# Hybrid decoder layer on one core: squares of x on two engines, S5 kernel blocks read inside the first rotation, S5 outputs copied by VectorE beside the o projection, one factor sum for two expert pairs

## The chip, the core and the metric

The kernel runs on one core of a Trainium2 chip. A core has a matrix engine (PE in the profile, with its weight loads as PEld), VectorE (DVE), ScalarE (ACT), GpSimd (POOL) and SyncE (SP, which here only starts transfers and waits). They share an on-chip memory; matrix results go to PSUM, eight banks of 128 partitions by 512 floats; DMA engines bring the weights from HBM. Each engine runs its own instructions in the order in which they were written and waits on semaphores for the others. The metric is the device time of the whole program in microseconds, lower is better.

## The reference, cut to what matters

One layer of a hybrid decoder, batch 1, 256 tokens, width 1024, all in float32.

```python
h    = rmsnorm(x, norm_mix_g)                       # (256, 1024)
p    = h @ w_in                                     # columns q | k | v | o (512 each) | i, f (4 each) | u (512)
A    = sigmoid(o) * headnorm(mlstm(silu(conv(q)), silu(conv(k)), v, i, f))      # 4 heads of 128
s_t  = abar * s_{t-1} + bbar @ u_t                  # S5: 32 groups of 16 channels, 64 complex states each
y    = gelu(Re(C s) + D u);  z = y @ glu_w + glu_b
B    = z[:16] * sigmoid(z[16:])                     # per group
x    = x + concat([A, B]) @ w_out
t    = rmsnorm(x, norm_ffn_g)
# top 1 of 4 groups, then top 2 of the 8 experts in it: weights combine[t, e]
x    = x + sum_e combine[:, e] * ((silu(t @ w_gate[e]) * (t @ w_up[e])) @ w_down[e])   # 32 experts, 1024 x 512
out  = rmsnorm(x, norm_final_g)
```

The 32 experts' weights are 201 MB of float32, and every one of them is read.

## The kernel before, in words

Nothing schedules the work: what is written first is issued first on each engine, and Python generators (`run` empties one, `next` takes one step) weave pieces of different parts into one order. `half(i)` is one of a set of 8 KB-per-partition slots of on-chip memory, `cst`, `mw` and `xs` are smaller areas, and `PS[:, bk, :]` is PSUM bank bk.

1. **Start.** x comes in two blocks of 128 tokens, `xs[:, 0]` and `xs[:, 1]`. Its squares are summed (L253 on VectorE for block 0; L262 and L263, one half each on VectorE and ScalarE, for block 1). GpSimd adds eps and takes the power -1/2 (L238 and L239 of `rpow`, then L265 and L266). PE transposes x meanwhile (L258), spreads the two factors over the columns (L275, L276), and VectorE writes the normalised, transposed h (L283). Projections that have h^T as the moving operand are `proj32T` (L433), with h as the stationary one `proj32N` (L441); u is the first of them.
2. **S5.** `transposeB(0)` and `(1)` (L494) transpose the input matrices four blocks at a time into a bank that VectorE, and for the fourth batch ScalarE, copies out (L497). `inputs_to_states` (L522, L524) and `kernelK` (L505) follow; the latter makes the blocks of the S5 kernel inside a chunk in bank 1. `rotate(0)` and `rotate(1)` (L577 to L597) turn the states of one half of the groups each, run the scans (L588) and turn them back (L589 to L597). Between them L600 to L603 read the kernel's blocks (`K4`, bank 1) into `KX`. `proj32N("v", (0, 1))` writes banks 0 and 1.
3. **mLSTM.** q, k, v and o are projected; `conv` does the short convolution (L531 on ScalarE, L535 on VectorE, SiLU L538). `prep` splits weights into a rounded high part (ScalarE, L422) and the rest (GpSimd or VectorE, L423), and `projN` makes a projection with three matmuls of the parts (L452, L454, L456) a quarter at a time, o into banks 5 and 7.
4. **S5 outputs.** `states_to_outputs` (L650) leaves the outputs transposed in banks 0 and 1; they are copied into `YT` (L703, one bank by ScalarE, the other by VectorE); `outputs_back` transposes them (L657) and ScalarE takes the GELU (L660). `glu(t)` is the per-group gate (L714 to L721). The scores (L666), `w_out` (L800), the residual, the second norm and the router follow.
5. **Experts.** They are done in 16 pairs. For each pair, one-hot matrices of the chosen tokens gather the inputs (L984), `wide` multiplies by gate, up and the last by down (L1011), `weigh` (L1017, L1018) scales and splits the result, and `scatter` (L1026) adds it into four banks. `factors` (L956 to L963) makes the gathered tokens' norm factors for the next pairs: two tiny matmuls and a sum over three columns per pair. It is called once for one pair and seven times for two.
6. **Weights.** `fetch(upto)` (L128 to L151) issues the expert weights on SyncE's queue (L150), 1 MB each for most, in the order of their use and into the slots that the steps before have freed; SyncE waits at each for the slot and for an older transfer.

Of the kernel before, what the change touches and what calls it, by code (L numbers as in the profile page):

```python
# [20 lines left out]
D = 1024  # L21
# [51 lines left out]
def tile_hymba(ctx, tc, x, norm_mix_g, w_in, conv_w, conv_b, i_bias, f_bias, mlstm_norm_g,  # L73
# [178 lines left out]
    flat = lambda t, c: t[:, c].rearrange("p b t -> p (b t)")  # L252
    STT(scr[:, 0, :], xs[:, 0, :], 1.0 / D, xs[:, 0, :], OP.mult, OP.mult, accum_out=ssq[:, 0:1])  # L253
    V.tensor_copy(ldt0[0:16], rowsA[0:16, 0:2])
# [5 lines left out]
    for _ in range(2):  # L260
        MM(PS[:, 0, 0:128], ident, ident, start=True, stop=True)
    STT(scr[:, 0, 0:512], xs[:, 1, 0:512], 1.0 / D, xs[:, 1, 0:512], OP.mult, OP.mult, accum_out=sh[:, 1, 0:1])  # L262
    ACT(scr[:, 1, 0:512], xs[:, 1, 512:], AF.Square, scale=1.0 / 32, accum_out=sh[:, 1, 1:2])  # L263
    rpow(ssq[:, 0:1], ssq[:, 0:1], 1.0, 1)
    G.tensor_scalar(ssq[:, 1:2], sh[:, 1, 0:1], sh[:, 1, 1:2], EPS, OP.add, OP.add)  # L265
    G.tensor_tensor(ssq[:, 1:2], ssq[:, 1:2], neg_half[:, 0:1], OP.pow)  # L266

    p = dict(zip(["dt", "lr", "lrdt", "mag", "th", "n", "r", "ab", "sin", "cos", "f", "hi", "lo", "den", "am1",
# [280 lines left out]
    load_w("o", (19, 21))  # L549
    for i in range(2):  # L550
        run(transposeB(i))
    run(inputs_to_states())
# [24 lines left out]
    def rotate(n):  # L577
        rs = slice(8 * n, 8 * n + 8)
        cT, sT, z, w = [t[:, rs] for t in (cosT, sinT, zr, zi)]
        a, b, c = [tt[:, i] for i in range(3)]  # L580
        TT(a, Vr[:, rs], cT, OP.mult)
        TT(b, Vi[:, rs], sT, OP.mult)
        TT(c, Vi[:, rs], cT, OP.mult)
        TT(w, Vr[:, rs], sT, OP.mult)
        TT(z, a, b, OP.add)
        TT(w, c, w, OP.subtract)
        for t in (z, w):
            V.tensor_tensor_scan(fl(t), fl(rho[:, rs]), fl(t), 0.0, OP.mult, OP.add)  # L588
        TT(a, z, cT, OP.mult)  # L589
        TT(b, w, sT, OP.mult)  # L590
        TT(c, z, sT, OP.mult)

        TT(z[:, :, 1:64], a[:, :, 0:63], b[:, :, 0:63], OP.subtract)
        TT(a, w, cT, OP.mult)
        TT(w[:, :, 1:64], a[:, :, 0:63], c[:, :, 0:63], OP.add)
        for t in (z, w):
            V.memset(t[:, :, 0:1], 0.0)  # L597

    rotate(0)
    TT(dd[0:32], fr(dsk[0:32], (1, 16), (0, 16)), fr(dl16[0:32], (0, 16), (1, 16)), OP.mult)  # L600
    TT(KX, fr(K4, (32, 16), (0, 2), (1, 16)), fr(mask2, (0, 16), (1, 2), (0, 16)), OP.mult)  # L601
    TT(dd2[0:32], fr(dd[0:32], (16, 16), (0, 2), (1, 16)), fr(mask2[0:32], (0, 16), (1, 2), (0, 16)), OP.mult)
    TT(KX[0:32], KX[0:32], dd2[0:32], OP.add)  # L603
    cv = conv(0, 2)
    qk = cuts(half(7), (8, 256))[0]
# [5 lines left out]
    prep(2)  # L611
    rotate(1)
    next(cv)
# [88 lines left out]
    for h in range(2):  # L702
        (V.tensor_copy if h else A.copy)(YT[:, h], PS[:, h, :].rearrange("p (q f) -> p q f", q=4))  # L703
    outputs_back()
# [24 lines left out]
    next(cv)  # L729
    for i in range(4):  # L730
        run(projN("o", (5, 7), i))
        if i == 0:
            for g in gated((0, 1)):
                run(g)
            for m in range(4):
                next(cv)
        if i == 1:
            next(cv)
        if i == 2:
            gl = gated((2, 3))  # L740
# [215 lines left out]
    def factors(js, bk):  # L956

        for j in js:
            at = PS[:, bk, 4 * j:4 * j + 3]
            for b in range(2):  # L960
                MM(at, oh[:, b, 2 * j:2 * j + 2].rearrange("p e s -> p (e s)"), rpt[:, b], start=b == 0, stop=b == 1,
                   skip_group_check=True)
            V.tensor_reduce(rp[:, j:j + 1], at, AX.X, OP.add)  # L963

# [376 lines left out]
```

## Time and profile before

| | |
|---|---|
| median of 3 runs | 615.29 us (614.74 to 617.84) |
| the profiled execution | 615.09 us |
| its span in the profile | 613.4 us, about 1.7 us lie around it |
| mean granted clock of PE | 0.992 |
| busy: PE, PEld, DVE, ACT, POOL | 582.2, 311.8, 226.4, 127.0, 58.1 us |
| chain that ended last | PE 90%, DVE 4%, ACT 2%, issue 1%, DMA 1%, POOL 1% |
| weights and rest read from HBM | 218.17 MB, 357 GB/s over the span |

The span runs from the first to the last instruction of the profiled execution, and all starts below are counted from it. The chain goes back from the last instruction, at each step to whatever released it. A timeline row gives start, duration and engine of one instruction, or of several of the same kind with their count, and in brackets how long the engine sat idle before it and what ended that. PE's records come in two per matmul of this precision, so an instruction of the program can be two records. Granted clock 1.00 is 2.4 GHz and 0.5 is 1.2 GHz.

### The profile page before, as it was taken

Reading aid. Unit: us, or ns where it says so; the run is one execution under the profiler, and the core shown is the slowest. Engines: PE = TensorE matmul, PEld = TensorE weight load, DVE = VectorE, ACT = ScalarE, POOL = GpSimd, SP = SyncE. Lnnn points to the kernel's source line nnn. Section 1 sums busy time; section 2 is a strip of 40 time slices with the busy share of each in tenths; the row PEclk is TensorE's granted clock in tenths of the full one; section 3 lists DMA queues with packets and bytes.
Section 4 is the critical chain, followed back from the end, with each engine's and each line's share of the span. In section 5 each row is a group of like instructions: output and inputs, shape, how many; then the busy total and the mean of one; then the engine's idle time right before and its main releaser. Section 6 shows DMA issues by size and latency. Waiting matters only on the chain.

```text
span 613.4 us, 8110 instructions
## 1 busy us (share of the span) xinstructions
PE 582.2 (95%) x3228; PEld 311.8 (51%) x3228; DVE 226.4 (37%) x589; ACT 127.0 (21%) x236; POOL 58.1 (9%) x74
## 2 busy tenths in 40 slices
PE   7999997999999999999999999999999999999993
PEld 6788486877743633363363335335433533444342
DVE  5969961685832311231322123132212313221133
ACT  3481647432411010000100010110001010101023
POOL 7040319050000000000000000000000000000003
PEclk9999998999999999999999999999999999999997
DMA  8791049299999999999999999999999999999992
GB/s 226 242 301 59 3 185 418 70 389 409 379 384 420 418 419 420 419 420 419 419 419 418 422 419 420 420 419 419 420 418 420 418 419 420 419 420 420 416 292 74
DMA packets 51337, 219.79 MB, mean 358 GB/s; under 512 B 15236, under 2 KB 20448, under 8 KB 27232
## 3 DMA queue, kind: packets, MB, share of 16 engines
q1 hardware_dynamic: 50800, 218.17, 88.7%
q10 hardware_dynamic: 496, 1.06, 0.5%
q8 instruction: 27, 0.44, 0.3%
q14 instruction: 14, 0.11, 0.0%
HBM read 218.17 MB, written 1.05 MB: 357 GB/s over the span
## 4 chain that ended last, share of the span: by engine, by line
PE 90%; DVE 4%; ACT 2%; issue 1%; DMA 1%; POOL 1%; POOLq 0%; DVEq 0%; ACTq 0%
PE psum L1011 55%; PE psum L984 6%; PE psum L433 6%; PE psum L1026 5%; PE psum L800 4%; PE psum L441 2%; PE psum L1149 2%; DMA xs<-in_x_dram 1%; PE psum L1030 1%; PE psum L452 1%; PE psum L650 1%; PE psum L454 1%; PE psum L456 1%; PE psum L463 1%; PE psum L494 1%
## 5 line engine op out<-in xcount | busy, mean ns | idle before, releaser
L1011 PE MATMUL psum<-half,mw 128*64 128x512 f32 x1504 | 330.0, 594 | 2.7 <-ACT mw L1151 1.5
L1011 PEld LDWEIGHTS psum<-half,mw 128*64 128x64 f32 x1504 | 105.0, 137 | 206.0 <-issue 198.5
L1018 DVE SCALAR_TENSOR_TENSOR Y<-psum,cst,Y 128x512 fp32r<-128x512 f32 x28 | 21.0, 751 | 129.2 <-ACT Y L1017 129.2
L1135 DVE SCALAR_TENSOR_TENSOR mw<-psum,cst,mw 128x512 f32<-128x512 f32 x16 | 12.0, 751 | 141.6 <-PE psum L1011 141.6
L1017 ACT ACTIVATE Y<-psum,cst 128x512 fp32r<-128x512 f32 x28 | 19.3, 688 | 195.8 <-PE psum L1011 133.6
L433 PE MATMUL psum<-half,half 128*128 128x256 f32 x192 | 42.4, 380 | 0.4 <-DVE half L283 0.4
L984 PE MATMUL psum<-cst,xs 128*128 128x256 bf16 (+1 forms) x384 | 40.9, 266 | 0.0
L1176 POOL MEMSET mw<- 128x2 f32 x1 | 0.1, 100 | 426.3 <-PE psum L1149 426.3
L984 PEld LDWEIGHTS <-xs 128*128 128x128 bf16 x384 | 40.0, 144 | 0.0
L433 PEld LDWEIGHTS psum<-half,half 128*128 128x128 f32 x192 | 36.2, 190 | 5.7 <-DVE half L283 0.6
L1026 PE MATMUL psum<-Y,Sc 128*128 128x512 f32 x112 | 33.6, 421 | 0.0
L1026 PEld LDWEIGHTS psum<-Y,Sc 128*128 128x128 f32 x112 | 18.8, 188 | 25.2 <-issue 22.7
L423 POOL TENSOR_TENSOR half<-half,half 128x1024 fp32r<-128x1024 f32 x10 | 24.5, 2466 | 63.6 <-ACT half L422 45.8
L1151 ACT COPY mw<-psum 128x256 f32<-128x256 f32 x15 | 5.6, 374 | 108.6 <-PE psum L1149 108.5
L967 DVE TENSOR_TENSOR mw<-psum,cst 128x512 f32<-128x512 f32 x32 | 22.0, 691 | 15.0 <-PE psum L984 8.8
L800 PE MATMUL psum<-half,half 128*128 128x512 f32 x96 | 24.3, 402 | 0.3 <-ACT half L828 0.3
L1128 ACT ACTIVATE mw<-psum,cst 128x512 f32<-128x512 f32 x16 | 11.0, 689 | 51.9 <-PE psum L1011 51.9
L800 PEld LDWEIGHTS psum<-half,half 128*128 128x128 f32 x96 | 17.5, 188 | 4.6 <-ACT half L828 0.5
L992 DVE TENSOR_SCALAR mw<-cst 128x64 f32<-128x64 f32 x64 | 15.6, 307 | 0.0
L441 PE MATMUL psum<-half,half 128*128 128x512 f32 x32 | 14.2, 595 | 1.5 <-DVE half L601 1.5
L1149 PE MATMUL psum<-ident,mw 128*128 128x128 f32 x64 | 11.7, 305 | 1.9 <-DVE mw L1135 1.9
L1151 DVE COPY mw<-psum 128x256 f32<-128x256 f32 x15 | 6.4, 425 | 18.8 <-ACT mw L1151 18.8
(351 smaller groups left out, 512.9 us busy)
## 6 DMA issues: line engine op xcount, KB each, us to landing
half<-in_expert_w_gate_dram SPq DMA_DIRECT2D x64, 1024.0 KB, 19.9
half<-in_expert_w_up_dram SPq DMA_DIRECT2D x64, 1024.0 KB, 19.9
half<-in_expert_w_down_dram SPq DMA_DIRECT2D x60, 1024.0 KB, 19.9
half<-in_w_in_dram SPq DMA_DIRECT2D x8, 1024.0 KB, 8.0
half<-in_w_out_dram SPq DMA_DIRECT2D x4, 1024.0 KB, 8.1
half<-in_expert_w_down_dram SPq DMA_DIRECT2D x6, 512.0 KB, 13.7
half<-in_w_in_dram SPq DMA_DIRECT2D x4, 512.0 KB
half<-in_expert_w_down_dram SPq DMA_DIRECT2D x4, 256.0 KB, 7.6
```

The lines of the kernel that those rows point to most:

```text
L423: es[i].tensor_tensor(rests[i], w, made[i].bitcast(F32), OP.subtract)
L433: MM(PS[:, bk + m // 2, 256 * (m % 2):256 * (m % 2) + 256], w[:, at:at + 128], flat(h32, c), start=c == 0 and m % 2 == 0, stop=c == 7, ski ...
L441: MM(PS[:, bks[b], :], h32[:, c, b], raw[g, c // 2][:, 512 * (c % 2):512 * (c % 2) + 512], start=c == 0, stop=c == 7, skip_group_check=True)
L800: MM(PS[:, WB[2 * b + i], :], m[:, k % 4, ts], w[:, 512 * i:512 * i + 512], start=False, stop=n == 7 and m is ml, skip_group_check=True)
L967: TT(xg[:, cs, ss], PS[:, bk, :].rearrange("p (c s) -> p c s", c=n), fr(g2[:, cs], (1, n), (0, m)), OP.mult)
L984: MM(PS[:, DN[f % 2], m * c:m * c + m], xp[:, k, b, n * f + c::8], oh[:, b].rearrange("p e s -> p (e s)")[:, ss], start=c == b == k == 0, ...
L992: TS(ow[:, b, e], places, rk[:, b, 2 * pr + e:2 * pr + e + 1], wt[:, b, 2 * pr + e:2 * pr + e + 1], OP.is_equal, OP.mult)
L1011: MM(PS[64 * e:64 * e + 64, bk, 0:w[e].shape[-1]], lhs[:, c, 64 * e:64 * e + 64], w[e], start=c == 0, stop=c == n - 1, skip_group_check=True)
L1017: ACT(hi, src, AF.Copy, scale=w)
L1018: STT(lo, src, w, hi.bitcast(F32), OP.mult, OP.subtract)
L1026: MM(PS[:, WB[2 * b + n], :], Sc[:, b], Y[:, k], start=False, stop=False, skip_group_check=True)
L1149: TR(PS[:, GB, 128 * c:128 * c + 128], act[:, c::4], ident)
```

## The change

It has four parts.

- The squares of both blocks of x are split: half of each on VectorE, the other half on ScalarE, and GpSimd handles each block right behind its own squares.
- One step of q's projection (`next(qs)`, four matmuls) stands between the two B transposes and no longer among those behind `transposeK`, and `rotate` becomes a generator that stops behind the scans: L600 to L603 are issued there, before the states are turned back.
- Both copies of the S5 outputs are VectorE's, and o's first quarter stands before the transposes back rather than behind them; the first gate (`gated((0, 1))`) now follows o's second quarter instead of its first.
- `factors` issues the matmuls of all its pairs into one bank and then sums once for all of them.

```diff
-    STT(scr[:, 0, :], xs[:, 0, :], 1.0 / D, xs[:, 0, :], OP.mult, OP.mult, accum_out=ssq[:, 0:1])
+    for b in range(2):
+        STT(scr[:, b, 0:512], xs[:, b, 0:512], 1.0 / D, xs[:, b, 0:512], OP.mult, OP.mult, accum_out=sh[:, b, 0:1])
+        ACT(scr[:, b, 512:], xs[:, b, 512:], AF.Square, scale=1.0 / 32, accum_out=sh[:, b, 1:2])
+        G.tensor_scalar(ssq[:, b:b + 1], sh[:, b, 0:1], sh[:, b, 1:2], EPS, OP.add, OP.add)
+        G.tensor_tensor(ssq[:, b:b + 1], ssq[:, b:b + 1], neg_half[:, 0:1], OP.pow)
...
-    STT(scr[:, 0, 0:512], xs[:, 1, 0:512], 1.0 / D, xs[:, 1, 0:512], OP.mult, OP.mult, accum_out=sh[:, 1, 0:1])
-    ACT(scr[:, 1, 0:512], xs[:, 1, 512:], AF.Square, scale=1.0 / 32, accum_out=sh[:, 1, 1:2])
-    rpow(ssq[:, 0:1], ssq[:, 0:1], 1.0, 1)
-    G.tensor_scalar(ssq[:, 1:2], sh[:, 1, 0:1], sh[:, 1, 1:2], EPS, OP.add, OP.add)
-    G.tensor_tensor(ssq[:, 1:2], ssq[:, 1:2], neg_half[:, 0:1], OP.pow)
...
-    for i in range(2):
-        run(transposeB(i))
+    run(transposeB(0))
+    next(qs)
+    run(transposeB(1))
...
         for t in (z, w):
             V.tensor_tensor_scan(fl(t), fl(rho[:, rs]), fl(t), 0.0, OP.mult, OP.add)
+        yield
         TT(a, z, cT, OP.mult)
...
-    rotate(0)
+    rot = [rotate(n) for n in range(2)]
+    next(rot[0])
     TT(dd[0:32], fr(dsk[0:32], (1, 16), (0, 16)), fr(dl16[0:32], (0, 16), (1, 16)), OP.mult)
     TT(KX, fr(K4, (32, 16), (0, 2), (1, 16)), fr(mask2, (0, 16), (1, 2), (0, 16)), OP.mult)
...
+    run(rot[0])
...
     for h in range(2):
-        (V.tensor_copy if h else A.copy)(YT[:, h], PS[:, h, :].rearrange("p (q f) -> p q f", q=4))
+        V.tensor_copy(YT[:, h], PS[:, h, :].rearrange("p (q f) -> p q f", q=4))
+    run(projN("o", (5, 7), 0))
     outputs_back()
...
-    for i in range(4):
+    for i in range(1, 4):
         run(projN("o", (5, 7), i))
-        if i == 0:
+        if i == 1:
             for g in gated((0, 1)):
...
-        for j in js:
-            at = PS[:, bk, 4 * j:4 * j + 3]
+        at = PS[:, bk, 0:8].rearrange("p (j k) -> p j k", j=2)
+        for n, j in enumerate(js):
             for b in range(2):
-                MM(at, oh[:, b, 2 * j:2 * j + 2].rearrange("p e s -> p (e s)"), rpt[:, b], start=b == 0, stop=b == 1,
-                   skip_group_check=True)
-            V.tensor_reduce(rp[:, j:j + 1], at, AX.X, OP.add)
+                MM(at[:, j, 0:3], oh[:, b, 2 * j:2 * j + 2].rearrange("p e s -> p (e s)"), rpt[:, b],
+                   start=n == b == 0, stop=b == 1, skip_group_check=True)
+        V.tensor_reduce(rp[:, js[0]:js[-1] + 1], at[:, js[0]:js[-1] + 1, 0:3], AX.X, OP.add)
```

On PE, around the B transposes (L494), the steps of q (L433, operand `half_6_106`) and the first half of v (L441), the order before is:

```order
12 L494 MATMUL psum<-ident,half_9_125 128x128 x16
13 L494 MATMUL psum<-ident,half_10_126 128x128 x16
...
78 L566 MATMUL psum<-ident,half_1_72 128x76
79 L433 MATMUL psum<-half_12_144,half_6_106 128x256 x4
80 L514 MATMUL psum<-ident,mw 128x128 x4
81 L433 MATMUL psum<-half_12_144,half_6_106 128x256 x12
82 L441 MATMUL psum<-half_7_118,half_12_144 128x512 x8
```

and after the change, where the lines are L492, L431 and L439:

```order
12 L492 MATMUL psum<-ident,half_9_125 128x128 x16
13 L431 MATMUL psum<-half_12_144,half_6_106 128x256 x4
14 L492 MATMUL psum<-ident,half_10_126 128x128 x16
...
79 L565 MATMUL psum<-ident,half_1_72 128x76
80 L431 MATMUL psum<-half_12_144,half_6_106 128x256 x4
81 L512 MATMUL psum<-ident,mw 128x128 x4
82 L431 MATMUL psum<-half_12_144,half_6_106 128x256 x8
83 L439 MATMUL psum<-half_7_118,half_12_144 128x512 x8
```

Four matmuls of q have moved in between the two sets of transposes, and eight instead of twelve stand directly ahead of v.

On VectorE, the first rotation before: the scans (L588), the turning back (L589 to L597), and then the kernel's blocks (L601 reads PSUM).

```order
100 L588 SCALAR_TENSOR_TENSOR half_28_563<-half_18_220,half_28_563 128x512 x2
101 L589 TENSOR_TENSOR half_27_562<-half_28_563,half_22_297 128x512
102 L590 TENSOR_TENSOR half_27_562<-half_28_563,half_22_297 128x512
103 L591 TENSOR_TENSOR half_27_562<-half_28_563,half_22_297 128x512
104 L593 TENSOR_TENSOR half_28_563<-half_27_562 128x8x63
105 L594 TENSOR_TENSOR half_27_562<-half_28_563,half_22_297 128x512
106 L595 TENSOR_TENSOR half_28_563<-half_27_562 128x8x63
107 L597 MEMSET half_28_563 128x8 x2
108 L600 TENSOR_TENSOR half_1_72<-cst 32x256
109 L601 TENSOR_TENSOR half_1_72<-psum,cst 128x512
```

After the change the scans are L587 and the reading of the blocks L602 to L605:

```order
99 L587 SCALAR_TENSOR_TENSOR half_28_564<-half_18_221,half_28_564 128x512 x2
100 L602 TENSOR_TENSOR half_1_72<-cst 32x256
101 L603 TENSOR_TENSOR half_1_72<-psum,cst 128x512
102 L604 TENSOR_TENSOR mw<-half_1_72,cst 32x512
103 L605 TENSOR_TENSOR half_1_72<-half_1_72,mw 32x512
104 L589 TENSOR_TENSOR half_27_563<-half_28_564,half_22_298 128x512
```

The four instructions of the kernel's blocks have moved ahead of the eight that turn the states back.

On PE, behind the last `states_to_outputs` (L650), before: the transposes back (L657) come first, then o's first quarter (twelve matmuls, of which the first three are shown) and the gate (L714).

```order
91 L650 MATMUL psum<-half_10_126,half_28_563 64x128 x16
92 L657 MATMUL psum<-ident,half_50_799 32x128 x32
93 L452 MATMUL psum<-half_30_607,half_16_216 128x512
94 L454 MATMUL psum<-half_31_608,half_16_216 128x512
95 L456 MATMUL psum<-half_30_607,half_17_217 128x512
...
105 L714 MATMUL psum<-half_50_799,half_2_73 128x256 x4
```

After the change, with L653, L450 to L454 and L660 for the same operations:

```order
92 L653 MATMUL psum<-half_10_126,half_28_564 64x128 x16
93 L450 MATMUL psum<-half_30_608,half_16_217 128x512
94 L452 MATMUL psum<-half_31_609,half_16_217 128x512
95 L454 MATMUL psum<-half_30_608,half_17_218 128x512
...
105 L660 MATMUL psum<-ident,half_50_800 32x128 x32
106 L450 MATMUL psum<-half_30_608,half_16_217 128x512
107 L452 MATMUL psum<-half_31_609,half_16_217 128x512
```

Twelve matmuls of o now stand between the states' outputs and their transposes back, and o's second twelve follow those transposes, ahead of the gate.

## Rows read from the trace of the kernel before

**Rows 1.** The page's part 4: shares of the chain that ended last, by line.
```profile
PE psum L1011 55%; PE psum L984 6%; PE psum L433 6%; PE psum L1026 5%; PE psum L800 4%; PE psum L441 2%; PE psum L1149 2%; DMA xs<-in_x_dram 1%; PE psum L1030 1%; PE psum L452 1%; PE psum L650 1%; PE psum L454 1%; PE psum L456 1%; PE psum L463 1%; PE psum L494 1%
```

**Rows 2.** Stretch: length, PE, PEld, DVE, ACT, POOL busy, granted clock, DMA share, GB/s.
```profile
core 0: us, PE busy (x) PEld busy (x) DVE busy (x) ACT busy (x) POOL busy (x), PEclk, DMA share, GB/s
...
101.20:104.70 3.50, 3.50 (x65) 3.12 (x58) 0.00 (x0) 1.86 (x4) 3.50 (x4) 0.51 1.01 414
...
164.00:170.00 6.00, 5.69 (x30) 2.26 (x32) 4.90 (x28) 0.78 (x6) 0.00 (x0) 1.00 0.77 285
170.00:592.00 422.00, 412.22 (x2134) 178.51 (x2130) 98.03 (x260) 39.50 (x64) 0.10 (x1) 1.00 1.01 417
592.00:613.00 21.00, 11.22 (x98) 7.92 (x94) 8.13 (x17) 6.78 (x21) 5.69 (x9) 0.84 0.36 113
```

**Rows 3.** The chain that ended last: start us, us, what; two periods of the expert loop.
```profile
214.13 10.45 PE psum L1011 x48
...
268.62 10.45 PE psum L1011 x48
```

**Rows 4.** Timeline around the first expert matmul (start us, us, engine line, operation, idle before).
```profile
155.10 13.22 SPq L150 DMA_DIRECT2D half<-in_expert_w_down_dram  x4
...
164.31 3.65 PE L1011 MATMUL psum<-half,mw 128*64 128x512 f32 x16 [0.54 <-DVE mw L967]
```

**Rows 5.** Timeline of the last weights.
```profile
590.09 0.69 ACT L1017 ACTIVATE half<-psum,cst 128x512 fp32r<-128x512 f32 x1 [5.80 <-DMA half<-in_expert_w_down_dram]
...
599.69 1.97 PE L1011 MATMUL psum<-half,half 128*64 128x128 f32 x32
```

**Rows 6.** Timeline, squares of x to the first projection.
```profile
5.53 1.23 DVE L253 SCALAR_TENSOR_TENSOR half<-xs 128x1024 f32<-128x1024 f32 x1 [2.96 <-DMA xs<-in_x_dram]
...
6.87 0.88 POOL L238 TENSOR_SCALAR cst<-cst 128x1 f32<-128x1 f32 x1 [0.79 <-DVE cst L254]
...
8.47 0.39 POOL L265 TENSOR_SCALAR cst<-cst 128x1 f32<-128x1 f32 x1
...
11.63 3.72 PE L433 MATMUL psum<-half,half 128*128 128x256 f32 x16 [0.37 <-DVE half L283]
```

**Rows 7.** Timeline, the B transposes on PE and the copy behind them.
```profile
39.88 2.20 PE L494 MATMUL psum<-ident,half 128*128 128x128 f32 x16 [0.91 <-DVE half L497]
...
42.11 0.59 ACT L497 COPY half<-psum 128x512 f32<-128x512 f32 x1 [1.51 <-PE psum L494]
```

**Rows 8.** Timeline, the first rotation to the k projection.
```profile
54.12 5.35 PE L433 MATMUL psum<-half,half 128*128 128x256 f32 x24
54.54 2.32 DVE L588 TENSOR_TENSOR_SCAN half<-half,half 128x512 f32<-128x512 f32 x2
...
61.09 0.67 DVE L601 TENSOR_TENSOR half<-psum,cst 128x512 f32<-128x512 f32 x1
...
61.81 13.14 PE L441 MATMUL psum<-half,half 128*128 128x512 f32 x30 [1.48 <-DVE half L601]
...
67.89 4.68 POOL L423 TENSOR_TENSOR half<-half,half 128x1024 fp32r<-128x1024 f32 x2 [29.39 <-ACT half L422]
...
71.08 2.04 DVE L585 TENSOR_TENSOR half<-half 128x512 f32<-128x512 f32 x1
```

**Rows 9.** Timeline, transposed S5 blocks (L505, L657) and the first gate matmuls (L714).
```profile
49.84 2.02 PE L505 MATMUL psum<-half,half 128*32 128x128 f32 x64
...
90.36 4.67 POOL L423 TENSOR_TENSOR half<-half,half 128x1024 fp32r<-128x1024 f32 x2 [17.79 <-issue]
...
100.37 0.59 ACT L703 COPY half<-psum 128x512 f32<-128x512 f32 x1
...
101.02 3.50 PE L657 MATMUL psum<-ident,half 128*32 128x128 f32 x64 [3.38 <-ACT half L703]
...
107.38 1.89 PE L714 MATMUL psum<-half,half 128*128 128x256 f32 x8
```

**Rows 10.** Waits: engine, line, releaser: us in total, times, longest us.
```profile
PE psum L961 <- DVE cst L963: 5.7, 7, 0.8
```

More of the change, by code (lines that the diff above doesn't have):

```diff
@@ L597, in rotate @@
             V.memset(t[:, :, 0:1], 0.0)
-    rotate(0)
+        yield
+    rot = [rotate(n) for n in range(2)]
+    next(rot[0])
     TT(dd[0:32], fr(dsk[0:32], (1, 16), (0, 16)), fr(dl16[0:32], (0, 16), (1, 16)), OP.mult)
@@ L611, in tile_hymba @@
     prep(2)
-    rotate(1)
+    run(rot[1])
     next(cv)
@@ L736, in tile_hymba @@
                 next(cv)
-        if i == 1:
+        if i == 2:
             next(cv)
-        if i == 2:
             gl = gated((2, 3))
```

## The prediction, made before the changed kernel had run

> **What bounds the kernel now.** I read the chain first, since a change can only pay where the end is set. More than half of it is one line, the experts' matmuls [rows 1], so the question is what an earlier or a shorter expert loop is worth. The table by stretch answers half of it: from 170 to 592 us the DMA engines are busy throughout at 417 GB/s, and PE is busy for 412.2 of the 422.0 us [rows 2]. Two things are nearly full at once. Which is the harder limit comes from their rates. PE repeats itself every 268.62 - 214.13 = 54.49 us [rows 3], in which it takes two pairs, four experts of 6.29 MB, 25.17 MB. The stream needs 25.17 MB / 417 GB/s = 60.4 us for that. So the stream is the slower of the two by 5.9 us per period; PE doesn't see it because it starts late, with slots full of weights, and eats that stock over the 7.7 periods from 164 to 583 us (some 45 us). In the tail the stock is gone: ScalarE sits 5.80 us until a w_down piece lands at 590 us, while PE's last gate and down matmuls run on without a wait in brackets [rows 5]. PE and the stream arrive together.
>
> That makes two ends to move. The stream after 170 us is dense and of fixed length, so it ends earlier only if it starts earlier. From 164 to 170 its share is 0.77 [rows 2]: SyncE takes 13.22 us, to 168.3, to issue four pieces, in order and each held until a slot is free, while the first expert matmuls, which free the first gate slot, start at 164.31 [rows 4]. So the dense stream is released by PE's first expert matmuls, and whatever the front of the kernel (0 to 164 us) gains goes through to the end. What PE gains inside the loop doesn't.
>
> **The change part by part.**
>
> *Squares of x.* Before, GpSimd's first step for block 0 starts at 6.87 and takes 0.88 us, where the same operation for block 1 takes 0.39 at 8.47; between them lie 0.72 us (8.47 - 7.75) for the power. The whole block on VectorE took 1.23 us [rows 6]; half of it is then about 0.65. The first step can start between 6.4 and 6.87, and that for block 1 at 6.4 to 6.87 + 0.39 + 0.72 = 7.5 to 8.0 instead of 8.47. That is 0.5 to 1.0 us for the first projection at 11.63, which waited 0.37 us for the chain behind it [rows 6]. I take 0.8; the bounds are 0 (the chain has another last part, u's weights or the S5 parameters) and 1.0.
>
> *A step of q between the transposes.* PE sat 0.91 us before the second transposes [rows 7]; the four matmuls are eight records of 5.35 / 24 = 0.22 us [rows 8], 1.8 us. They fill the 0.91 and push the second transposes by 0.9, which the 0.8 above pays for. Queued behind is ScalarE's copy at 42.11 [rows 7] and then its exponentials for the gates, which come some 0.1 us later in absolute time than now, or 0.9 later if the first edit yields nothing. The same 1.8 us are missing later ahead of v, so PE gains the 0.91 (bounds 0.4 and 1.4).
>
> *Kernel blocks inside the rotation.* The first v matmuls that need bank 1 wait 1.48 us for L601, which stands behind the turning back: it runs at 61.09, though the scans end at 54.54 + 2.32 = 56.86 [rows 8]. Behind the scans it ends at about 56.86 + 0.4 + 0.67 = 57.9, less what the front gained. PE reaches v at 54.12 + 5.35 - 1.8 = 57.7 and has two matmuls for bank 0 first, so the wait goes: 1.48. What is late next are the states, 1.9 us later (four instructions, moved ahead of them), but before they are used PE has 13.1 us of v and then k. To here PE is 0.8 + 0.91 + 1.48 = 3.2 us earlier (bounds 2.0 and 3.7).
>
> A second gain lies beside it. L585 took 2.04 us at 71.08, where another VectorE operation of 128x512 took 0.67; GpSimd's L423 ran from 67.89 to 72.57 [rows 8]. L423 waits for a ScalarE chain behind L601 to L603 and moves up by about 3.6 us, to an end near 69, before L585. I count 1.3 us for VectorE from there. The Trainium skill, SBUF — State Buffer, section "SBUF: two separate sides", gives the mechanism: a VectorE instruction with two on-chip operands and a GpSimd instruction take one shared port pair for the whole instruction, and the loser stands still. The 2.04 us agree with it. By that rule the collision can also only move to another such instruction; then the 1.3 us are not gained, and o's first quarter, below, starts later by about as much.
>
> *S5 outputs and o.* Before, PE is idle 3.38 us until ScalarE's copy at 100.37, then L657 takes 3.50 us, to about 104.5, and the first gate starts at 107.38, so a quarter of o takes about 2.9 [rows 9]. The 3.50 is at a granted clock of 0.51, the 1.2 GHz level [rows 2]; the same form takes 2.02 us at L505 [rows 9]. After the change the states' outputs end at 101.02 - 3.38 - 3.2 = 94.4. o's first quarter needs banks that ScalarE frees behind GpSimd's L423, which ended at 90.36 + 4.67 = 95.03 [rows 9] and ends near 93.7 with the 1.3 us above; with an exponential of about 0.6 (the size of the copy L703) that is 94.3. So PE goes on without a stop: 2.9 of o, in which VectorE makes both copies (twice 0.7), 2.0 for L657 at full clock, 2.9 of o's second quarter, and the gate starts at 94.4 + 7.8 = 102.2. That is 5.2 us earlier than 107.38, and PE has one quarter (2.9 us) less to do behind it. Behind the gate come the taps and SiLUs of VectorE and ScalarE, which hold the scores, so most of those 2.9 us become waiting: bounds 0 and 2.9, and I take 0.8, nearer to the chain that stays. The first expert matmul is then 5.2 + 0.8 = 6.0 us earlier, at 158.3 (bounds 4.0 and 7.5).
>
> *Factors.* Seven times PE waits for VectorE's sum between two pairs' tiny matmuls, 5.7 us in total [rows 10]. One sum takes that away: the loop on PE gets shorter by 5.7. By the rates above it is not worth that. PE comes to the tail with the stock used up earlier, and the last weights land when the stream brings them. What is gained is the distance that PE still had to the last landings; no row prices it, so the bounds are 0 and 5.7. I take 0.6, since ScalarE already waits 5.80 us for a landing there [rows 5].
>
> Sum against the profiled execution: 615.09 - 6.0 - 0.6 = 608.5 us. The median of the runs shown is 0.2 above that execution.
>
> **The rivals.**
>
> *PE bounds to the end.* If the stream can run faster than 417 GB/s or has more stock than I think, the 5.7 us are seen in full: 615.09 - 6.0 - 5.7 = 603.4. For it: PE is busy 98% of the loop and leads the chain [rows 1, 2]. Against it: DMA share 1.01 for 422 us. Chance 0.10.
>
> *The front gives less.* VectorE stays blocked (1.3 less), the exponentials late by the q step (0.9 less), and nothing of PE's spare quarter (0.8 less): 608.5 + 3.0 = 611.5. It is of the same kind as the forecast and needs most of these at once. Chance 0.17 for 610 to 612.
>
> *The stream isn't released by PE.* If something else sets when the dense stretch starts, only the 0.6 remains: 614.5. Against it speak the 0.77 and SyncE's 13.22 us [rows 2, 4]. Chance 0.10.
>
> *Slower: PE starves and loses its clock.* PE will now wait for weights in the tail. Before 101.2 an idle of 3.38 us was followed by a granted clock of 0.51, and the work took 3.50 / 2.02 = 1.73 times as long [rows 2, 9]. In the last 21 us the clock is 0.84 already [rows 2]. If the last pairs ran at the 1.2 GHz level, each us of work would cost 0.73 more; to end 3.1 us later than now it must eat 6.6 + 3.1 = 9.7 us, which is 13 us of PE work. The end then comes at 618 or later. The Trainium skill, TensorE: Matmul & The Clock Gate, section "HAM oscillation — how this bites in real kernels", describes exactly this, waits for transfers between blocks of matmuls that bring the clock down each time. Against it: the lag of the stream is 5.9 us in a period of 24 pieces, so a wait is about 0.25 us per piece, and the 0.91 us of idleness before the second transposes [rows 7] lie in a stretch, 0 to 43 us, whose granted clock is 1.00 [rows 2]. Chance 0.04.
>
> **How the numbers follow.** The forecast, 607 to 610, has 0.59, and the four rivals 0.10, 0.17, 0.10 and 0.04. The measurement tells about 0.5% (3.1 us) from no change, so faster means under 612.2, slower over 618.4: faster 0.59 + 0.10 + 0.16 = 0.85, same 0.11, slower 0.04. The range leaves out the third and the fourth rival and about half of the first, 0.19 in all: 605.0 to 612.3.
>
> **What would show it.** Right: v on PE without a break at L601; no idle PE and a granted clock of 1.00 around the transposes back; the first gate near 102 and the first expert matmul near 158; no wait at `factors`; and small new waits of PE for w_gate, w_up or w_down in the last two pairs, with a stretch of dense DMA as long as before. Wrong: a first expert matmul less than 4 us earlier, an end that moves by over 10 us, or a reduced clock in the loop.

## The result, and the profile after

The changed kernel takes 607.96 us (median of 4 runs, 607.72 to 609.25), the kernel before 615.84 (4 runs, 614.74 to 617.84): ratio 0.9868, 95% interval 0.9842 to 0.9893. The forecast was 608.5. The profiled execution took 607.72 us with a span of 606.0, against 615.09 and 613.4 before.

Shares of the chain that ended last, by engine and by line, of the kernel after:

```profile
PE 46%; DMA 40%; DVE 6%; issue 4%; ACT 2%; POOL 1%; POOLq 0%; SPq 0%; DVEq 0%; ACTq 0%
PE psum L1014 25%; DMA half<-in_expert_w_down_dram 13%; DMA half<-in_expert_w_gate_dram 13%; DMA half<-in_expert_w_up_dram 13%; PE psum L431 4%; PE psum L803 4%; PE psum L987 3%; PE psum L1029 2%; DVE mw L533 2%; DMA xs<-in_x_dram 1%; POOL half L421 1%; PE psum L1152 1%; PE psum L1033 1%; PE psum L810 1%; PE psum L461 1%
```

This answers [rows 1]: PE's 90% have become 46%, and 40% are now weights, in three equal parts (gate, up, down). So for 40% of the span the end hangs on the stream. The table by stretch, with the columns in its first line:

```profile
core 0: us, PE busy (x) PEld busy (x) DVE busy (x) ACT busy (x) POOL busy (x), PEclk, DMA share, GB/s
...
94.00:100.70 6.70, 6.58 (x84) 5.31 (x85) 1.95 (x4) 6.61 (x14) 6.70 (x5) 1.00 1.04 422
...
158.00:164.00 6.00, 6.00 (x32) 2.20 (x30) 4.90 (x30) 0.78 (x6) 0.00 (x0) 1.00 0.94 337
164.00:586.00 422.00, 416.68 (x2139) 180.84 (x2136) 96.73 (x250) 39.44 (x64) 0.10 (x1) 1.00 1.01 417
586.00:606.00 20.00, 9.63 (x88) 7.07 (x87) 7.71 (x16) 6.78 (x21) 5.68 (x9) 0.87 0.36 111
```

To be read beside [rows 2]: the 1.2 GHz stretch at 101 is gone, the DMA share in the 6 us around the first expert matmul has risen from 0.77 to 0.94, and then the stream is as dense as before, at the same 417 GB/s. The chain (start us, us, what) shows the period and the place where it changes over:

```profile
206.50 10.45 PE psum L1014 x48
...
260.03 10.45 PE psum L1014 x48
...
278.65 19.84 DMA half<-in_expert_w_gate_dram
...
499.62 19.88 DMA half<-in_expert_w_up_dram
```

The period of two pairs is 260.03 - 206.50 = 53.53 us; before it was 54.49 [rows 3]. From 278.65 to 519.50 us the chain goes from one weight's issue to its landing and on to the next, some 20 us each: PE waits for nothing there, but a faster PE would have ended no earlier. PE's waits (us in total, times, longest):

```profile
PE psum L1014 <- DMA half<-in_expert_w_up_dram: 1.3, 1, 1.3
```

The 5.7 us of [rows 10] are gone altogether, and one wait for a weight has appeared; it ends at 519.54, where the chain above goes back to PE, earlier than the last two pairs in which it was expected. Behind it the chain runs along PE to the end. A weight still comes late there: ScalarE's scaling in `weigh` is idle until a w_down lands.

```profile
582.30 0.69 ACT L1020 ACTIVATE half<-psum,cst 128x512 fp32r<-128x512 f32 x1 [6.79 <-DMA half<-in_expert_w_down_dram]
```

That was 5.80 us before [rows 5]. In the front, the squares of x and the first projection:

```profile
6.47 0.58 POOL L256 TENSOR_SCALAR cst<-cst 128x1 f32<-128x1 f32 x1 [0.41 <-ACT half L255]
...
7.79 0.30 POOL L256 TENSOR_SCALAR cst<-cst 128x1 f32<-128x1 f32 x1
...
10.99 4.37 PE L431 MATMUL psum<-half,half 128*128 128x256 f32 x19 [0.37 <-DVE half L281]
```

The first projection is at 10.99 instead of 11.63 [rows 6]. The B transposes:

```profile
38.16 1.89 PE L431 MATMUL psum<-half,half 128*128 128x256 f32 x8
...
39.89 1.91 PE L492 MATMUL psum<-ident,half 128*128 128x128 f32 x16
...
41.83 0.58 ACT L495 COPY half<-psum 128x512 f32<-128x512 f32 x1 [1.89 <-PE psum L492]
```

The step of q fills the hole, and the copy behind is 0.28 us earlier than before [rows 7]. The rotation and v:

```profile
56.83 0.67 DVE L603 TENSOR_TENSOR half<-psum,cst 128x512 f32<-128x512 f32 x1
...
57.27 13.90 PE L439 MATMUL psum<-half,half 128*128 128x512 f32 x32
...
63.63 4.67 POOL L421 TENSOR_TENSOR half<-half,half 128x1024 fp32r<-128x1024 f32 x2 [25.80 <-ACT half L420]
...
70.82 0.68 DVE L584 TENSOR_TENSOR half<-half 128x512 f32<-128x512 f32 x1
71.01 4.26 PE L431 MATMUL psum<-half,half 128*128 128x256 f32 x19
```

v (L439) runs without a break from 57.27, and k starts at 71.01 instead of about 74.8; GpSimd's pass ends at 68.3, and the VectorE instruction that took 2.04 us [rows 8] takes 0.68. The S5 outputs:

```profile
93.47 0.60 ACT L690 ACTIVATE half<-psum 128x512 f32<-128x512 f32 x1 [0.36 <-POOL half L421]
...
94.12 0.50 PE L450 MATMUL psum<-half,half 128*128 128x512 f32 x1 [0.27 <-ACT half L690]
...
94.67 1.28 DVE L706 COPY half<-psum 128x512 f32<-128x512 f32 x2
...
97.07 1.96 PE L660 MATMUL psum<-ident,half 128*32 128x128 f32 x64
...
101.81 1.89 PE L718 MATMUL psum<-half,half 128*128 128x256 f32 x8
```

o's first quarter begins as the exponential that frees its bank ends (93.47 + 0.60), the transposes back take 1.96 us at full clock, and the gate starts at 101.81 instead of 107.38 [rows 9]. The first expert matmul:

```profile
148.42 13.23 SPq L150 DMA_DIRECT2D half<-in_expert_w_down_dram  x4
...
157.64 3.65 PE L1014 MATMUL psum<-half,mw 128*64 128x512 f32 x16 [0.53 <-DVE mw L970]
```

It is 6.67 us earlier than before [rows 4], and SyncE again takes 13.2 us for the four issues ahead of it.

### The profile page after: what moved, and what is told of

Same layout as the page of the kernel before. It is cut to its first block, busy times and chain, and to the rows that moved or that the text cites. A ratio compares the mean times of both kernels' runs of the same rounds, so it can differ in the third digit from the quotient of the medians.

```text
span 606.0 us, 8112 instructions
## 1 busy us (share of the span) xinstructions
PE 585.0 (97%) x3228; PEld 312.8 (52%) x3228; DVE 224.2 (37%) x583; ACT 127.3 (21%) x237; POOL 57.5 (9%) x74
## 4 chain that ended last, share of the span: by engine, by line
PE 46%; DMA 40%; DVE 6%; issue 4%; ACT 2%; POOL 1%; POOLq 0%; SPq 0%; DVEq 0%; ACTq 0%
PE psum L1014 25%; DMA half<-in_expert_w_down_dram 13%; DMA half<-in_expert_w_gate_dram 13%; DMA half<-in_expert_w_up_dram 13%; PE psum L431 4%; PE psum L803 4%; PE psum L987 3%; PE psum L1029 2%; DVE mw L533 2%; DMA xs<-in_x_dram 1%; POOL half L421 1%; PE psum L1152 1%; PE psum L1033 1%; PE psum L810 1%; PE psum L461 1%
## 5 line engine op out<-in xcount | busy, mean ns | idle before, releaser
L1014 PE MATMUL psum<-half,mw 128*64 128x512 f32 x1504 | 334.0, 596 | 4.0 <-ACT mw L1154 1.5
L1014 PEld LDWEIGHTS psum<-half,mw 128*64 128x64 f32 x1504 | 106.4, 137 | 210.0 <-issue 193.6
L1020 ACT ACTIVATE Y<-psum,cst 128x512 fp32r<-128x512 f32 x28 | 19.2, 687 | 189.1 <-PE psum L1014 126.9
L431 PE MATMUL psum<-half,half 128*128 128x256 f32 x192 | 42.6, 380 | 0.4 <-DVE half L281 0.4
L431 PEld LDWEIGHTS psum<-half,half 128*128 128x128 f32 x192 | 36.1, 190 | 5.7 <-DVE half L281 0.6
L970 DVE TENSOR_TENSOR mw<-psum,cst 128x512 f32<-128x512 f32 x32 | 22.0, 691 | 15.0 <-PE psum L987 13.1
L439 PE MATMUL psum<-half,half 128*128 128x512 f32 x32 | 13.9, 592 | 0.0
```

The costliest lines, as they stand in the source:

```text
L431: MM(PS[:, bk + m // 2, 256 * (m % 2):256 * (m % 2) + 256], w[:, at:at + 128], flat(h32, c), start=c == 0 and m % 2 == 0, stop=c == 7, ski ...
L439: MM(PS[:, bks[b], :], h32[:, c, b], raw[g, c // 2][:, 512 * (c % 2):512 * (c % 2) + 512], start=c == 0, stop=c == 7, skip_group_check=True)
L970: TT(xg[:, cs, ss], PS[:, bk, :].rearrange("p (c s) -> p c s", c=n), fr(g2[:, cs], (1, n), (0, m)), OP.mult)
L1014: MM(PS[64 * e:64 * e + 64, bk, 0:w[e].shape[-1]], lhs[:, c, 64 * e:64 * e + 64], w[e], start=c == 0, stop=c == n - 1, skip_group_check=True)
L1020: ACT(hi, src, AF.Copy, scale=w)
```

## The experiments

Each has a profiled execution. The table gives the start of the first expert matmul in it, the time from there to the end of the span, the places before the last ten us at which the granted clock was near 0.5, and the medians (the kernel before was run again beside each group).

| run | first expert matmul | from there to the end | near 1.2 GHz at | median | before, same chip |
|---|---|---|---|---|---|
| before | 164.31 | 449.1 | 101 | 615.84 | |
| after | 157.64 | 448.4 | 556 | 607.96 | 615.84 |
| d1_delay_front | 162.25 | 447.8 | 562 | 612.35 | 616.43 |
| d2_delay_loop | 157.36 | 448.1 | nowhere | 608.11 | 616.43 |
| h1_half_gates | 164.01 | 448.5 | 101 | 617.04 | 616.43 |
| h2_half_gates_factors | 164.06 | 443.4 | 102, 559 | 609.72 | 616.43 |
| e1_factors_only | 162.63 | 448.1 | 563 | 613.72 | 615.95 |
| e3_s5_only | 160.47 | 448.9 | nowhere | 612.66 | 615.95 |
| e6_q_kx_only | 161.71 | 449.1 | 99 | 614.35 | 615.95 |
| e8_x_only | 161.74 | 448.5 | nowhere | 614.69 | 615.95 |
| e4_copies_only | 159.37 | 452.1 | 562 | 613.07 | 616.51 |
| e5_order_only | 160.77 | 451.6 | 563 | 614.27 | 616.51 |
| e7_kx_only | 163.69 | 450.5 | 98, 566 | 613.91 | 616.51 |
| e9_fill_idle | 162.50 | 451.3 | 565 | 615.57 | 616.51 |

**What sets the end: the same work put at two places.** The edit, in the changed kernel, with pr 0 for the first run and 4 for the second:

```diff
+        if pr == 0:
+            for _ in range(24):
+                MM(PS[:, GB, 0:128], ident, ident, start=True, stop=True)
         for c in range(8):
             wide(GB, xin, c, 8, ...)
```

d1_delay_front: 

> The changed kernel with 24 extra matmuls of the identity (128x128, results not used), about 24 x 0.22 = 5.3 us of PE work, directly ahead of the first expert's gate matmuls. Theory S (the first expert matmul releases the weight stream, and the end follows the stream): the first gate matmul for weights at 157.6 + 5.3 = 162.9, the dense stretch of DMA as long as in the changed kernel and 5.3 us later, time 607.9 + 5.3 = 613.2. Theory P (the end follows the sum of PE's work): 613.2 as well. Theory R (the stream is started by something else): no more than 1 us over 607.9.

d2_delay_loop: 

> The changed kernel with the same 24 extra matmuls ahead of the gate matmuls of pair 4, inside the expert loop. Theory S: PE has about 35 us of weights in stock there and gets the 5.3 us back from its waits in the tail; it arrives with 0.5 to 1.5 us to spare or missing, so 607.9 + 0 to 1.0. Theory P: 613.2, as with the same work in front of the loop. Theory R: 613.2, as P.

PE's timeline in the first, and the inserted row of the second:

```profile
156.75 5.58 PE L1114 MATMUL psum<-ident 128*128 128x128 f32 x48
162.25 1.94 PE L1014 MATMUL psum<-half,mw 128*64 128x512 f32 x8
```

```profile
266.71 5.62 PE L1114 MATMUL psum<-ident 128*128 128x128 f32 x48
```

Both inserted blocks take 5.6 us. In front of the loop the block moves the first expert matmul by 4.61 us, 0.65 less than expected: it starts in the 0.53 us in which PE waited before, and the first projection of this execution was 0.27 early. The median moves by 4.4 (612.35 against 607.96, measured in another group). Inside the loop the block moves the median by 0.15, less than the runs of one kernel differ; the span is 605.5, and PE has no wait for a weight any more. Against the kernel before of their own group the ratios are 0.9935 (0.9912 to 0.9959) and 0.9871 (0.9835 to 0.9907). Theory S stands, P and R fall: P needed 613 for the second run, R needed no change for the first.

**The stream made shorter.** Half of each gate piece is read, from the 47th transfer on, and the matmuls use that half twice (the output is then not the reference's). The second run has the new `factors` as well.

```diff
+            if kind == 0 and n >= 2 * NP:
+                parts = [(w[:, 0:2], parts[0][1][:, 0:2])]
...
-            place[order[n]] = w
+            place[order[n]] = Twice(w) if kind == 0 and n >= 2 * NP else w   # index c % 2 for c
```

h1_half_gates: 

> The kernel before, but from the 47th weight transfer on each gate piece is read half (512 KB), and its matmuls read that half twice, so the output is not the reference's; PE's work is the same, the stream is some 25 MB (60 us) shorter. Theory S: the stream is no limit any more, only PE is; that is worth only what the tail lost before, 0 to 1 us: 614.3 to 615.3. Theory P: 615.3.

h2_half_gates_factors: 

> The kernel before with half of the gate weights as in the run ahead, and with the new factors alone of the four edits. Theory S: with the stream out of the way the 5.7 us of waits show in full: 5.7 us below the run ahead, 608.6 to 609.6. A rival, that the waits at factors were covered by something on PE's own path: within 1 us of the run ahead.

The stretch from 170 to 540 us of each, columns as above (lengths, busy times, clock, DMA share, GB/s):

```profile
170.00:540.00 370.00, 362.35 (x1890) 159.32 (x1887) 88.28 (x236) 34.05 (x55) 0.00 (x0) 1.00 0.97 394
```

```profile
170.00:540.00 370.00, 367.58 (x1920) 161.09 (x1918) 87.80 (x231) 33.99 (x55) 0.00 (x0) 1.00 0.98 398
```

PE's busy time in these 370 us rises from 362.35 to 367.58: the waits are gone. From the first expert matmul to the end it is 448.5 and 443.4 us; with a full stream it was 449.1 before and 448.1 with `factors` alone. So the sum per two pairs is worth 1.0 us with the full stream and at least 5 us with the short one: the clock fell at 559 in h2 and not in h1, and the same piece of PE's work there (L1153 to the next sixteen matmuls of L1020) took 15.57 us in h2 and 14.46 in h1. The medians differ by 7.3, and h2's is 0.1 above its range. h1's span is 0.9 us under that of before. Its median, 617.04, is above its range; the ratio of 1.0006 has an interval from 0.9982 to 1.0030, 1.1 us faster to 1.8 slower. The last w_down landed 38 us earlier in h1 than before (562.1 against 600.0), and the end came less than 1 us earlier, as little as with a shorter PE alone: in the kernel before, the two limits end together.

**Each edit alone, on the kernel before.**

```diff
e1   only the new factors
e3   only: V.tensor_copy for both YT halves, o's first quarter ahead of outputs_back()
e6   only: next(qs) between the transposes, rotate split, KX behind the scans
e8   only: the split squares of x
```

e1_factors_only: 

> The kernel before with the factors edit alone. Theory S (the end follows the weight stream): PE's waits of 5.7 us at factors go, PE waits as much for weights in the last pairs, and the end moves by 0.4 to 1.0 us: 614.2 to 615.0. Theory P (the end follows PE): 5.7 us less, 609.6.

The first expert matmul came 1.68 us earlier, though nothing ahead of it differs from before: in this execution the transposes back took 1.95 us. From there to the end it is 1.0 us less than before. The median fell by 2.2, more than expected; its ratio, 0.9972 with an interval from 0.9946 to 0.9997, allows 0.2 to 3.3 us and so also the 0.4 to 1.0 of theory S, but not the 5.7 of theory P.

e3_s5_only: 

> The kernel before with the S5 edit alone (both copies on VectorE, o's first quarter ahead of the transposes back). Theory S: PE's 3.38 us of idleness and the 1.2 GHz stretch go, the first gate comes 2.0 us earlier less what o's first quarter waits for its bank, the first expert matmul 2.0 to 3.0 us earlier, the end as much plus 0: 612.3 to 613.4. Rival (the gain of the changed kernel at this place needed the earlier edits, since GpSimd's pass L423 holds the bank): the first gate less than 1 us earlier, 614.3 or more.

The first expert matmul is 2.16 us earlier than in e1 (the same front, full clock) and 3.84 earlier than before (1.2 GHz there). The gate is at 105.19, 2.2 earlier than before but only 0.4 earlier than in e1. The time, 612.66, is in the range.

e6_q_kx_only: 

> The kernel before with the second edit alone (a step of q between the B transposes, kernel blocks read inside the rotation). Theory S: v ends 3.0 us earlier, GpSimd's L423 no longer holds up VectorE (L585 0.7 instead of 2.0 us); in the region behind, the copy on ScalarE at 100.37 moves only by what VectorE and GpSimd gain, 1.4 us, and the 3.38 us of idle PE grow by the difference; first expert matmul 1.4 to 3.0 us earlier, 612.3 to 613.9. Rival (all of it is passed on): 612.0 or less.

v ends at 71.71 (3.2 us earlier), the transposes back start 2.66 earlier, and the first expert matmul 2.60 earlier, both executions with the clock down at the transposes. The span, 610.8, is 2.6 shorter, and the profiled execution, 612.47, lies in the range; the median, 614.35, is 1.6 shorter and 0.4 above the range. PE's idleness before the transposes grew by 0.6 us, from 3.38 to 3.96. Nearly all is passed on, though the rival's 612.0 isn't reached.

e8_x_only: 

> The kernel before with the split squares alone. Theory S: the first projection 0.64 us earlier as in the changed kernel; PE then waits 0.6 us longer for the kernel's blocks on VectorE unless these come earlier too, which they do since they follow PE's transposes; 614.6 to 615.1 against 615.3. Rival (the gain is eaten at the wait for the kernel's blocks or at the S5 copies): 615.3, v not earlier.

The first projection is at 10.67. Against e1 (same clock): 0.84 earlier there, 0.86 at the end of v, 0.86 at the gate, 0.89 at the first expert matmul. All of it goes through; the rival falls. The median, 614.69, is in the range.

**The parts of the S5 edit and of the rotation edit, and the clock.**

```diff
e4   only: V.tensor_copy for both YT halves
e5   only: run(projN("o", (5, 7), 0)) ahead of outputs_back(), copies as before
e7   only: rotate split, KX behind the scans
e9   before outputs_back():
+    for _ in range(13):
+        MM(PS[:, 6, 0:128], ident, ident, start=True, stop=True)
```

e4_copies_only: 

> The kernel before with both copies of the S5 outputs on VectorE, and o's first quarter still behind the transposes back. Theory S: the second copy ends near 98.3, the transposes back start there instead of at 101.02 and run at full clock (2.0 us), the gate is at 98.3 + 2.0 + 2.9 = 103.2 to 103.6, 3.8 to 4.2 us earlier than before; PE keeps about 0.7 us of idleness; first expert matmul 160.3 to 161.5, end at 448.4 plus that. A rival (the copying engine matters little; it's o's quarter beside the copies that pays): gate later than 105, first expert matmul at 162 or later.

e5_order_only: 

> The kernel before with o's first quarter ahead of the transposes back, and the copies one each on ScalarE and VectorE as before. Theory S: o's first quarter runs from 97.5 to 100.3 inside the old idleness, PE then waits 0.7 us for ScalarE's copy that ends at 100.97; L657 from 101.0 at full clock, o's second quarter, gate at 105.9, first expert matmul 160.8 to 161.5 (0.4 to 0.8 later than with both halves of the edit), end 448.4 later. A rival (without VectorE's copy there is no gain): first expert matmul at 162.6 or later, the value of the kernel before at full clock.

Timelines of e4 and of e3, both edits together:

```profile
96.77 0.69 DVE L703 COPY half<-psum 128x512 f32<-128x512 f32 x1 [0.45 <-PE psum L650]
...
97.53 1.95 PE L657 MATMUL psum<-ident,half 128*32 128x128 f32 x64
...
102.29 1.97 PE L714 MATMUL psum<-half,half 128*128 128x256 f32 x8
```

```profile
97.49 0.50 PE L452 MATMUL psum<-half,half 128*128 128x512 f32 x1
...
100.45 1.95 PE L657 MATMUL psum<-ident,half 128*32 128x128 f32 x64
...
105.19 1.89 PE L715 MATMUL psum<-half,half 128*128 128x256 f32 x8
```

With VectorE's copies alone the transposes back start at 97.53, as soon as the first copy is done, and the gate is at 102.29: better than forecast, and earlier than with o's first quarter ahead of them (105.19). The first expert matmul is at 159.37, 160.77 with the order alone, 160.47 with both, against 162.63 without either (all four at full clock there; e5's front ran 0.3 us early). So on the kernel before the copies give 3.3 us by themselves, and o's quarter in front of the transposes takes 1.1 of that back. ScalarE shows where, first e4, then e3:

```profile
101.76 1.21 ACT L660 ACTIVATE half<-psum 128x256 f32<-128x256 f32 x4
...
110.87 1.28 ACT L538 ACT_TABLE_LOAD   x1 [1.96 <-DVE mw L535]
```

```profile
101.72 1.42 ACT L660 ACTIVATE half<-psum 128x256 f32<-128x256 f32 x4
...
112.07 1.28 ACT L538 ACT_TABLE_LOAD   x1 [1.96 <-DVE mw L535]
```

The GELU (L660) starts at the same time in both. With VectorE's copies no idleness of PE is left there to fill; the quarter in front only puts the gate behind one more quarter of o, and what follows the gate, down to the SiLUs (L538), comes 1.2 us later. In e5 the rival falls too: the order alone is worth 1.6. Neither ended at 448.4 behind its first expert matmul (452.1 and 451.6); the reason stands below.

e7_kx_only: 

> The kernel before with the kernel blocks read inside the rotation, and all of q's steps where they were. Theory S: PE reaches v at 59.3 as before and doesn't wait for bank 1, so v ends 1.5 us earlier (73.4); VectorE and GpSimd gain as with the whole edit (L585 0.7 us), so the S5 copies and the first expert matmul are 1.0 to 2.6 us earlier. A rival (the step of q does the work): v no more than 0.5 us earlier.

v ends at 73.17, 1.8 us earlier (the rival falls), and the transposes back start 1.8 earlier. The first expert matmul is only 0.6 earlier, less than the 1.0 to 2.6 expected: in this execution the clock was down from 98.3 to 105.1, twice as long as before (101.2 to 104.6). The interval of its ratio, 0.9947 to 1.0009, doesn't exclude that the time is the same.

e9_fill_idle: 

> The kernel before with 13 extra matmuls of the identity (results not used) ahead of the transposes back, where PE is idle for 3.38 us. Theory S on the clock: with PE busy in the gap L657 runs at full clock, 2.0 instead of 3.5 us, and the gate, the first expert matmul and the end come 1.5 to 1.7 us earlier in every execution, though nothing else is changed: gate 105.7, first expert matmul 162.6, 611 to 613.5 with a narrower spread over the runs than the kernel before. A rival (the long L657 isn't due to the idleness): gate 107.4 as before.

Gate at 105.51 and first expert matmul at 162.50, as expected: 1.81 earlier than before, 0.24 of it because the whole front ran early (first projection at 11.39). So the fall of the clock costs 1.6 us at this place. The end missed its range: the median is 615.57 (ratio 0.9979, interval 0.9948 to 1.0011) and not 611 to 613.5, and the runs, 614.54 to 618.75, were about as far apart as the ten of e5, 612.03 to 616.97. The span was 613.8: this execution lost the clock elsewhere, at 565.

**Why medians and profiles differ.** Behind the same 3.38 us of idleness the transposes back, in e1, h1, e8 and e7 (the count and shape are the same):

```profile
100.89 1.95 PE L657 MATMUL psum<-ident,half 128*32 128x128 f32 x64 [3.38 <-ACT half L703]
```

```profile
100.70 3.55 PE L666 MATMUL psum<-ident,half 128*32 128x128 f32 x64 [3.38 <-ACT half L712]
```

```profile
100.02 1.96 PE L655 MATMUL psum<-ident,half 128*32 128x128 f32 x64 [3.38 <-ACT half L701]
```

```profile
99.23 3.64 PE L661 MATMUL psum<-ident,half 128*32 128x128 f32 x64 [3.38 <-ACT half L707]
```

Two executions at full clock, two near 1.2 GHz, though the four programs do the same work there. That the executions of one program differ too shows in the mean granted clock on record for every run: in the 88 runs of the kernel before beside these groups it goes from 0.978 to 0.994, and the span from 620.3 to 611.6 us with it (median 611.7 in the seven runs at 0.994, 615.4 in the nineteen from 0.985 to 0.988, 619.1 in the seven up to 0.981). In the 22 runs of after, d1 and d2 it is 0.991 to 0.996. A second such place is at pair 14. PE in e4, then its stretches there, and the same stretch of before and of after:

```profile
559.18 2.04 PE L1144 MATMUL psum<-cst,ident 8*128 8x128 f32 x16
561.16 0.75 PE L1149 MATMUL psum<-ident,mw 128*128 128x128 f32 x4
561.74 0.38 PE L999 MATMUL psum<-ident,mw 128*128 128x128 f32 x2
562.83 11.34 PE L1011 MATMUL psum<-half,mw 128*64 128x512 f32 x38 [0.70 <-DVE mw L1151]
```

```profile
540.00:561.00 21.00, 21.00 (x104) 8.46 (x100) 3.77 (x8) 2.06 (x3) 0.00 (x0) 1.00 1.01 421
562.00:568.40 6.40, 5.70 (x16) 1.71 (x16) 1.98 (x7) 0.32 (x1) 0.00 (x0) 0.50 1.02 419
```

```profile
562.00:570.00 8.00, 7.30 (x44) 4.24 (x42) 3.42 (x9) 0.96 (x2) 0.00 (x0) 1.00 1.02 420
```

```profile
555.90:560.00 4.10, 3.61 (x15) 1.84 (x16) 2.14 (x8) 0.96 (x2) 0.00 (x0) 0.58 1.01 420
```

Behind sixteen matmuls with only 8 partitions in use (L1144 before), a few small ones and a short wait, the clock was at 0.50 for 6.4 us in e4 and didn't fall at all in before; no run shows which of them brings it down. Where it falls and `factors` is the old one (e4, e5, e7, e9), the time from the first expert matmul to the end is 450.5 to 452.1 us; with the old one and no fall (before, e3, e6, e8) 448.5 to 449.1. With the new one it is 447.8 to 448.4 in all, whether it fell (after, d1, e1) or not (d2). The four falls with the old one are all of the last group, on another chip than the two groups ahead of it, so the chip is a rival as cause. The landing of the last w_down speaks against it: it comes 434.5 to 436.1 us behind the first expert matmul in all twelve traces with the full stream, whatever the chip. The span ends 12.4 to 13.4 us behind that landing in the other eight, and 14.9 to 17.4 in these four: the weights were in time, and PE came late.

## Why the prediction was right

*The bound.* Right, and shown by d1 and d2: a first expert matmul 4.61 us later costs 4.4 us, 5.6 us of work in the loop cost 0.15. The 434.5 to 436.1 us from there to the last landing, in every trace with the full stream, show the fixed length that the prediction assumed. PE had some 5 us in hand in the loop, the waits that `factors` no longer has.

*Squares of x.* 0.8 forecast, 0.64 in the pair of profiles, 0.84 to 0.89 in e8 against e1. The first projection starts at 11.25 to 11.63 in the ten traces without the edit and at 10.66 to 10.99 in the four with it, 0.72 apart in the mean. Right.

*q step and kernel blocks.* 0.91 + 1.48 forecast, 3.2 with the squares. k started 3.8 us earlier, just beyond the upper bound of 3.7, and e6 gives 3.2 without the squares: more than the two terms, by about 0.8. e7 shows 1.8 for the blocks, so the step is worth 1.4 rather than 0.9. The step's term was too low: its 1.8 us pushed the second transposes by 0.65 (39.89 against 39.88 before, with a front that is 0.64 early) and not by the 0.9 counted, and these then took 1.91 us instead of 2.20. VectorE's 1.3 us came as forecast (L584, 0.68 us at 70.82, with GpSimd's pass done at 68.3). The rule of the Trainium skill, SBUF — State Buffer, section "SBUF: two separate sides", agrees.

*S5 outputs and o.* The gate came at 101.81 against 102.2 forecast. The sum was right, but not its reason: it gave the credit to both halves of the edit, o's quarter filling the idleness and VectorE's copies ending in its shade. On the kernel before, e4 shows that the copies do it alone, since they leave no idleness to fill, and that the quarter ahead of the transposes only delays the gate and what hangs on it. Of the gain, 1.6 us are the clock, and those only in executions of the kernel before in which it fell. Behind the gate 1.1 us more were gained, 0.8 forecast.

*First expert matmul.* 6.0 forecast, 6.67 measured.

*Factors.* 0.6 forecast. It is 0.73 in the pair of profiles and 1.0 in e1. That it came so near is partly luck: the prediction had no row for it and took a value near the lower end of 0 to 5.7. What the forecast didn't see is what else it buys: where the clock falls at pair 14, the old `factors` pays 1.5 to 3.5 us for it and the new one nothing. That fits the runs of the changed kernel and of d2, which lie within 607.2 and 609.9, while those of before reach from 613.3 to 622.1 and are the longer the lower their mean clock. How often it falls at which place can't be counted, since only one execution of each kernel has a trace.

*The rivals.* "PE bounds to the end" is what h2 makes true by taking the stream away, and only then. "The front gives less" and "not released by PE" are refuted by the table. The slow rival was half right in the wrong place: the clock did fall in the tail of the changed kernel, at 556 to 560, not from waits for weights, and it cost nothing that can be seen: the last w_down landed 13.1 us before the end there and 13.4 in d2, whose clock didn't fall. PE's one long wait for a weight, the 1.3 us that end at 519.54, left the clock at 1.00 (first row below, of after); the loss at each transfer that the Trainium skill, TensorE: Matmul & The Clock Gate, section "HAM oscillation — how this bites in real kernels", describes is in none of these traces. As no matmul in them waits longer than 1.3 us for a weight, they hardly put it to the test. The second row is of before and has the front's granted clock, 1.00, which the prediction used and whose row was not shown:

```profile
519.00:524.00 5.00, 4.46 (x18) 1.72 (x18) 0.70 (x1) 0.00 (x0) 0.00 (x0) 1.00 1.01 419
```

```profile
0.00:43.00 43.00, 38.22 (x203) 31.88 (x204) 32.72 (x114) 23.58 (x48) 20.26 (x42) 1.00 0.84 248
```

*Left open.* Whether the changed kernel with o's first quarter back behind the transposes is faster still; e3 and e4 point to it (1.1 us at the first expert matmul without the other edits). It wasn't run.

## What to carry to other kernels

When two resources run side by side near their limits, compare their periods, not their busy shares, and the stock with which the faster one starts: the stream took 60.4 us per period against PE's 54.5, and the stock made both end together. Shortening either alone then brought 1 us or less, and both together 5 or more. An edit is then worth what it does ahead of the point that releases both. Time saved on the faster one isn't lost, though: it covers what disturbs that engine later. And an edit with two halves should be run as halves, since the sum can be right with one half working against the other.

## What was not expected of the hardware

The granted clock falls at places that differ from trace to trace, although the work there is the same: at the S5 copies in 5 of the 7 traces with the 3.38 to 3.96 us of idleness unfilled, and near pair 14 in 8 of 14 traces, for 3.4 to 6.8 us at either place. What decides it is not shown. One fall moves the time by 1.6 us at the first place and by up to 3.5 at the second if nothing covers it, as much as any edit here.
